# The last tile's output projection on its own plan of loads and operands

## Chip, core and metric

The kernel runs on one core of a Trainium2 chip. The metric is the device time of one execution in microseconds (us). The kernel before was timed three times: 2693.33 us in the median, 2690.28 to 2696.13. The engines are named as in the profile: PE multiplies matrices, DVE and ACT work on vectors, POOL on vectors too, SP issues DMA transfers.

## What is computed

Two mixers over 2048 rows of 1024 channels in float32: a gated MLP, then chunked attention with a shared K and V, a final output projection with a residual add, and an RMS norm. Only the last lines matter here:

```python
o = jnp.moveaxis(o, 0, 1).reshape(bsz, s, B_WIDTH)   # attention output, 16 heads of 64
return (o * jax.nn.silu(z)) @ w_out                  # gate, then output projection 1024 x 1024
...
x = x + chunk_attention_mixer(...)                   # residual
return rms_norm(x, final_norm_g)                     # final norm
```

## The kernel before

**Tiles.** The 2048 rows are four tiles t = 0..3 of 512 rows. In the attention part a tile goes through eight head pairs p = 0..7, each pair through eight steps u (`score`, `flip`, and `value` for each head). The output projection of tile t is done while tile t + 1 goes through its pairs: it is PE's filler work between the steps. `ahead(t, p)` (L1617) hands out this filler in small steps, by the table `SHARE`: in pair 7 of tile 3 it gives the last 12 steps of tile 2's projection and then the first 13 of tile 3's. What is left of tile 3's projection runs alone at the very end (L1693).

**Precision.** Each float32 operand is split in a high and a low part (`fp32r`), and a product is three matmuls (`mm3`, L112): high x high, left high x right low, left low x right high, at L113, L114 and L115. `split_s` (L291) splits a left operand: ACT copies the high part (Sho), DVE subtracts (Slo).

**Strassen.** The projection of a tile is one level of Strassen: seven products in the order `PHS = (1, 7, 2, 6, 5, 4, 3)`, each for two row halves jp, so 14 products of 12 matmuls. One product is four steps of filler. `o_right` (L228) brings a product's weights (two tiles q, each a high and a low part of 512 KiB, from the DRAM tensor `ows`), for tile 3's products 2, 3 and 5 from unsplit tensors instead, with the split on ACT and DVE (`split_in`, L209 and L210). All weight tiles lie in the eight places of tag `T`; a product needs four, so a load waits until the product before last has finished. `strassen` (L260) asks for left operands one product ahead and, for tile 3, for weights one product ahead.

**Left operands of tile 3.** `last_open` (L1456) loads quarters `00`, `10`, `01`, `11` of the attention output, as far as they exist, and POOL forms the sums s1 to s4. The last pairs come straight from `last_og` (L1486), when `value` has ended; products 2, 5, 4, 3 and 6 need pair 7.

**Eviction.** `o_evict` (L1502) takes a finished product out of PSUM. Products 1 and 7 are copied to x and y tiles; 2 and 5 are added to residual half rows (`resid`, 256 KiB each), 6 changes x and y; 4 and 3 close a half row. `done` squares on ACT; when a row block b has both halves, `finish(b)` makes the norm factor (two DVE adds, a POOL power) and `scale` multiplies and stores. For tile 2 the rows go through DRAM (`x2d`) and come back into one place (`y`, tag `bx`); its `finish` and `scale` wait in the list `finals`, from which one is taken per step u of pair 7, the rest before the last projection runs (L1691).

**Order.** The order on each engine is laid down when the program is built, by a planner that ranks instructions by their place in the program and lets one go when its operands and a place for its result are there in the planner's own reckoning; `on_beat` and the like add an order edge by hand. SP issues its loads strictly in that order: one that waits holds up all behind it.

Of the kernel before, what the change touches and what calls it, by code (L numbers as in the profile page):

```python
# [33 lines left out]
def trunk_kernel(  # L34
# [193 lines left out]
    def o_right(t):  # L228
        def right(ph):
            out = []  # L230
            for q in range(2):
                name = f"bo{t}_{ph}_{q}"
                if t + 1 == NT and ph in (2, 3, 5):
                    raw = raw_w(t, f"raw_{name}")
                    w = [w_tile(f"w{i}_{name}") for i in "hl"]
                    nc.sync.dma_start(raw[:], owf[q][:] if ph == 5 else wb_out[1, ph - 2, q])
                    split_in(raw, *w)
                else:
                    w = [w_tile(f"w{i}_{name}") for i in "hl"]
                    for i in range(2):  # L240
                        nc.sync.dma_start(w[i][:].bitcast(F32), ows[ph, q][:, i, :])
                out.append(w)
            return out
        return right
# [46 lines left out]
    def split_s(pool, bufs, name, src):  # L291
        hi, lo = (
            pool.tile([P, 4, P], F32R, tag="S", name=f"S{i}{name}", bufs=bufs) for i in "hl"
        )
        nc.scalar.copy(hi[:], src)
        tv(lo[:], src, hi[:].bitcast(F32), op=sub)
        return [(hi[:, k, :], lo[:, k, :]) for k in range(4)]
# [920 lines left out]
    with ExitStack() as bctx:  # L1218
# [200 lines left out]
        def o_left(t):  # L1419
            a = {}  # L1420
            if t + 1 == NT:
                return last_left

# [62 lines left out]
        def last_og(p, og32, z):  # L1486
            k = p - 4
            o4 = og32[:].rearrange("p (j r s) -> p r j s", j=2, r=2)
            z4 = z[:].rearrange("p (j r s) -> p r j s", j=2, r=2)
            for r in range(2):  # L1490
                nc.vector.scalar_tensor_tensor(
                    v4(la[f"{r}1"])[:, k], o4[:, r], 0.5, z4[:, r], op0=ALU.mult, op1=ALU.mult
                )
            if p == 7:
                for f_ in last_sums(slice(768, 1024)):
                    f_()

        def last_left(ph, jp):
            n = {1: "00", 7: "s3", 2: "01", 6: "s2", 5: "s1", 4: "11", 3: "s4"}[ph]
            return split_s(sb, 4, f"o_{ph}_{jp}", v4(la[n])[:, :, jp, :])  # L1500

        def o_evict(t):  # L1502
# [7 lines left out]
            def place(r, c, jp):  # L1510
                if not last:
                    return c_tile(f"oc{t}_{r}{c}{jp}")[:]
                b = 2 * jp + r
                if b not in row:
                    row[b] = sb.tile([P, 2, 512], F32, tag="K", name=f"row{b}", bufs=4)
                return row[b][:, c, :]
# [17 lines left out]
            def finish(b):  # L1534
# [4 lines left out]
                if last:  # L1539
                    y = row[b]  # L1540
                else:
                    on_beat(first)
                    y = sb.tile([P, 2, 512], F32, tag="bx", name=f"y{t}_{b}", bufs=1)
                    nc.sync.dma_start(y[:].rearrange("p a b -> p (a b)"), x2d[t][b][:])

                def scale():
                    for c in range(2):
                        cs = slice(c * 512, c * 512 + 512)
                        ins = nc.vector.scalar_tensor_tensor(
                            y[:, c, :], y[:, c, :], r[:], gf[:, cs], op0=ALU.mult, op1=ALU.mult  # L1550
# [4 lines left out]
                        nc.sync.dma_start(out[r0 : r0 + P, cs], y[:, c, :])  # L1555
# [6 lines left out]
            def evict(ph, jp, ps):  # L1562
# [6 lines left out]
                if ph in (2, 5):  # L1569
                    r = 0 if ph == 2 else 1  # L1570
                    c = place(r, r, jp)
                    resid(r, r, jp, c)
                    tv(c, ps, c, op=add)
                    tg(c, c, x_ if ph == 2 else y_, op=add)
                    done(r, r, jp, c)
                    if ph == 5:
                        tv(x_, ps, x_, op=add)
                        for r, c, y in ((1, 0, y_), (0, 1, x_)):
                            o = c_tile(f"or{t}_{r}{c}{jp}")[:]
                            resid(r, c, jp, o)  # L1580
                            tg(y, y, o, op=add)
                elif ph == 6:
                    tv(x_, ps, x_, op=add)
                    tg(y_, y_, x_, op=add)
                else:
# [6 lines left out]
        def o_all(t):  # L1592
            yield from strassen(
                f"bo{t}", o_right(t), o_left(t), o_evict(t), (t + 1) // NT
            )

        outs = [o_all(t) for t in range(NT)]
# [19 lines left out]
        def ahead(t, p):  # L1617
# [8 lines left out]
            else:  # L1626
                if t + 1 < NT:
                    reload(t + 1)
                yield from some(outs[t - 1], SHARE[t][p])
# [61 lines left out]
        while finals:  # L1691
            finals.pop(0)()
# [58 lines left out]
```

## Time and profile before

| | us |
|---|---|
| median of three runs | 2693.33 |
| profiled execution | 2698.01 |
| its span | 2696.2 |
| PE busy in the span | 2627.2 |
| end of PE's last matmul, from the span's start | 2687.78 |

Times in the profile's rows count from the start of the span. A timeline row gives start, duration, engine, line and operation, output and inputs, and in brackets the idle time ahead of it with what ended it. A row of stages gives the stretch, its length, busy time of PE, PE's weight loads, DVE, ACT and POOL with the number of instructions, then the granted PE clock, the DMA engines' busy share and GB/s. `bo` is the PSUM tile of an output product, `wh_bo` and `wl_bo` its weights, `pv`, `tp` and `s` belong to the attention, `row` is a residual row block of tile 3, `or` a residual half row, `ou` an x or y tile.

### The profile page before, as it was taken

How to read it: one execution, taken by the hardware profiler on the slowest of the kernel's cores; microseconds unless marked ns; L12 is line 12 of the kernel's file. 1: busy time of each engine (PE TensorE's matmuls, PEld its weight loads, DVE VectorE, ACT ScalarE, POOL GpSimd, SP SyncE). 2: the span in 40 equal slices, each digit the busy share in tenths (PEclk: the TensorE clock that was granted, in tenths of full speed). 3: DMA queues.
4: the chain of work that ended last, by engine and by line, in shares of the span. 5: the costliest groups of instructions: out<-in, count | busy, mean ns of one | idle time of the engine just before them, and what ended most of it. 6: DMA issues, size and time to landing. Idle time of an engine off the chain costs nothing.

```text
span 2696.2 us, 38071 instructions
## 1 busy us (share of the span) xinstructions
PE 2627.2 (97%) x12960; PEld 2197.9 (82%) x12960; DVE 1892.0 (70%) x2937; ACT 1296.6 (48%) x2296; POOL 888.2 (33%) x874
## 2 busy tenths in 40 slices
PE   9999999999999999999989999999999999999997
PEld 7888888888888888888878788787887888788885
DVE  5655676766777568657677767788677667766676
ACT  5422242443434435333365466676556555655553
POOL 3511335152262414015043344343332223323243
PEclk9999999999999999999999999999999999999999
DMA  7898999989888879858666687788889667766576
GB/s 293 314 326 332 342 364 326 328 306 350 331 320 281 308 259 334 301 200 273 256 238 209 216 266 232 223 294 290 281 265 295 200 220 246 242 204 193 180 236 238
DMA packets 274770, 735.53 MB, mean 273 GB/s; under 512 B 29584, under 2 KB 61328, under 8 KB 274576
## 3 DMA queue, kind: packets, MB, share of 16 engines
q1 hardware_dynamic: 274576, 733.09, 79.2%
q8 instruction: 104, 1.70, 0.2%
q14 instruction: 90, 0.74, 0.1%
HBM read 540.56 MB, written 181.93 MB: 268 GB/s over the span
## 4 chain that ended last, share of the span: by engine, by line
PE 81%; DVE 7%; DMA 6%; issue 2%; ACT 2%; POOL 2%; SPq 1%; DVEq 0%; POOLq 0%; ACTq 0%
PE P L115 11%; PE P L114 11%; PE P L113 11%; PE pj L115 5%; PE pj L113 5%; PE pj L114 5%; PE pv L1391 4%; PE Po L113 4%; PE Po L114 4%; PE Po L115 4%; PE s L1331 4%; PE tp L1366 3%; PE vp L115 1%; PE vp L113 1%; PE vp L114 1%
## 5 line engine op out<-in xcount | busy, mean ns | idle before, releaser
L113 PE MATMUL P<-T,S 128*128 128x512 f32 x1248 | 497.0, 398 | 2.1 <-ACT S L393 2.1
L115 PE MATMUL P<-T,S 128*128 128x512 f32 x1248 | 491.1, 394 | 0.0
L114 PE MATMUL P<-T,S 128*128 128x512 f32 x1248 | 490.1, 393 | 0.6 <-DVE T L396 0.6
L1350 POOL TENSOR_SCALAR pr<-pr,sl 128x640 f32<-128x640 f32 (+4 forms) x256 | 199.3, 779 | 522.9 <-DVE sl L1349 473.8
L113 PE MATMUL pj<-hh_b,wh_b 128*128 128x512 f32 x768 | 320.6, 417 | 1.6 <-ACT hh_b L168 0.8
L115 PE MATMUL pj<-hh_b,wl_b 128*128 128x512 f32 x768 | 305.9, 398 | 0.8 <-DVE wl_b L210 0.7
L114 PE MATMUL pj<-hl_b,wh_b 128*128 128x512 f32 x768 | 304.4, 396 | 0.0
L1346 ACT ACTIVATE pr<-pr,nm 128x640 f32<-128x640 f32 (+4 forms) x256 | 195.4, 763 | 193.2 <-DVE nm L1339 182.4
L115 PEld LDWEIGHTS P<-T,S 128*128 128x128 f32 x1248 | 235.8, 189 | 50.4
L113 PEld LDWEIGHTS P<-T,S 128*128 128x128 f32 x1248 | 236.2, 189 | 46.9 <-ACT S L393 2.3
L114 PEld LDWEIGHTS P<-T,S 128*128 128x128 f32 x1248 | 236.0, 189 | 46.1 <-DVE T L396 1.0
L1371 DVE TENSOR_TENSOR pt<-tp,pt 128x640 fp32r<-128x640 f32 (+4 forms) x256 | 188.7, 737 | 49.2 <-ACT pt L1370 46.2
L1339 DVE CUSTOM_DVE_ANT_0 pr<-s,bias 128x640 f32<-128x640 f32 (+4 forms) x256 | 188.0, 735 | 43.6 <-PE s L1331 36.7
L1370 ACT CAST pt<-tp 128x640 fp32r<-128x640 f32 (+4 forms) x256 | 159.1, 622 | 50.9 <-PE tp L1366 47.3
L1366 PE MATMUL tp<-ident,pr 128*128 128x128 f32 x1120 | 167.8, 276 | 10.4 <-DVE pt L1371 7.9
L115 PEld LDWEIGHTS pj<-hh_b,wl_b 128*128 128x128 f32 x768 | 145.5, 189 | 34.1 <-DVE wl_b L210 2.8
L1366 PEld LDWEIGHTS tp<-ident,pr 128*128 128x128 f32 x1120 | 131.4, 141 | 44.6 <-issue 17.0
L113 PEld LDWEIGHTS pj<-hh_b,wh_b 128*128 128x128 f32 x768 | 146.5, 191 | 20.1 <-ACT wh_b L209 1.6
L1391 PEld LDWEIGHTS pv<-pt,V 128*128 128x128 f32 x896 | 144.2, 190 | 20.2 <-ACT pt L1370 2.6
L114 PEld LDWEIGHTS pj<-hl_b,wh_b 128*128 128x128 f32 x768 | 146.6, 191 | 17.1
L1391 PE MATMUL pv<-pt,V 128*128 128x256 f32 (+3 forms) x896 | 154.4, 321 | 2.7 <-ACT pt L1370 1.8
L210 DVE TENSOR_TENSOR wl_b<-raw_b,wh_b 128x1024 fp32r<-128x1024 f32 x96 | 125.8, 1311 | 26.9 <-ACT wh_b L209 25.3
(283 smaller groups left out, 5739.4 us busy)
## 6 DMA issues: line engine op xcount, KB each, us to landing
S<-hsd SPq DMA_DIRECT2D x288, 512.0 KB, 5.4
rw<-in_w_a SPq DMA_DIRECT2D x108, 512.0 KB, 6.3
A<-ytd SPq DMA_DIRECT2D x72, 512.0 KB, 5.8
raw_b<-wk SPq DMA_DIRECT2D x72, 512.0 KB, 4.4
hsd<-S SPq DMA_DIRECT2D x56, 512.0 KB, 4.3
V<-vhd SPq DMA_DIRECT2D x56, 512.0 KB, 5.7
wh_bo<-ows SPq DMA_DIRECT2D x50, 512.0 KB, 4.7
wl_bo<-ows SPq DMA_DIRECT2D x50, 512.0 KB, 5.8
```

Source lines behind the costliest of these rows:

```text
L113: first = mm(ps, lh, rh, start=first, stop=False)
L114: mm(ps, lh, rl, start=False, stop=False)
L115: mm(ps, ll, rh, start=False, stop=last)
L210: tv(wl[:], raw[:], wh[:].bitcast(F32), op=sub)
L1331: mm(ps[:, sg, :w], q[:, qb * P : (qb + 1) * P], kx[:, koff + sg * w : koff + (sg + 1) * w], start=i == 0, stop=i == 1,)
L1339: nc.vector.tensor_tensor_reduce(out=pr[:, c0:].rearrange("p (a b) -> p a b", a=nseg), in0=ps[:, :nseg, :w], in1=bias[:, c0:].rearrange("p ...
L1346: nc.scalar.activation(pr[:, c0:], pr[:, c0:], AF.Exp, scale=-1.0, bias=nm[:], accum_out=sl[:])
L1350: nc.gpsimd.tensor_scalar(pr[:, c0:], pr[:, c0:], sl[:], 1.0, op0=ALU.mult, op1=ALU.mult)
L1366: ins = tpose(tp[:, b, :], pr[:, b * P : (b + 1) * P], ident[:])
L1370: nc.scalar.copy(oh, tp[:, b0:5, :].rearrange("p a b -> p (a b)"))
L1371: nc.vector.tensor_tensor(pt[:, 2560 + o + b0 * P : 2560 + o + 640], tp[:, b0:5, :].rearrange("p a b -> p (a b)"), oh.bitcast(F32), op=ALU ...
L1391: mm(po[:, q0 * P : q1 * P], vtl[t, p][:, i, hs], rhs, start=(i == blocks[0] and j == 0), stop=(i == 7 and j == 1),)
```

## The change

Tile 3's projection leaves the shared `strassen` and gets a generator of its own, `last_all`, with a hand-written table of what is asked for at which product.

- Weights: products 1, 7, 6 and 4 stay in the `T` places. Product 5 goes into the two `V` places (free when `value` of pairs 6 and 7 has ended), product 3 into the one `PT` place (free after the last `value`), both from the split tensors, so with no `split_in`; product 2 alone is still loaded unsplit, and split into the four `raw` places. Product 1 is asked for six steps before tile 2's projection ends (`last_first`).
- Left operands are asked for two products ahead and lie in the eight `Q` places instead of four `S`. If product 2's first one is asked for before pair 7 is there, three quarters of it are split at once and the last when `last_og` has run (`owed`).
- The residual comes as four whole row blocks (512 KiB, `last_row`) into `K` places, asked for at the third and fourth of the 14 products. The block of quarter 11 gets its y at product 6 instead of at product 5.
- Tile 2's `finals` are no longer emptied before the last projection; what is left is taken one by one from the sixth of the 14 products on. Row block 0 of tile 2 comes back into two half places of tag `og`.

```diff
     def o_right(t):
...
-                if t + 1 == NT and ph in (2, 3, 5):
-                    raw = raw_w(t, f"raw_{name}")
-                    w = [w_tile(f"w{i}_{name}") for i in "hl"]
-                    nc.sync.dma_start(raw[:], owf[q][:] if ph == 5 else wb_out[1, ph - 2, q])
-                    split_in(raw, *w)
-                else:
-                    w = [w_tile(f"w{i}_{name}") for i in "hl"]
-                    for i in range(2):
-                        nc.sync.dma_start(w[i][:].bitcast(F32), ows[ph, q][:, i, :])
+                w = [w_tile(f"w{i}_{name}") for i in "hl"]
+                for i in range(2):
+                    nc.sync.dma_start(w[i][:].bitcast(F32), ows[ph, q][:, i, :])
...
-    def split_s(pool, bufs, name, src):
+    def split_s(pool, bufs, name, src, tag="S", parts=None):
...
+        def part(ks):
+            nc.scalar.copy(hi[:, ks], src[:, ks])
+            tv(lo[:, ks], src[:, ks], hi[:, ks].bitcast(F32), op=sub)
+
+        if parts is None:
+            part(slice(0, 4))
+        else:
+            part(slice(0, 3))
+            parts.append(lambda: part(slice(3, 4)))
...
             if p == 7:
+                closed.append(p)
+                while owed:
+                    owed.pop(0)()
                 for f_ in last_sums(slice(768, 1024)):
                     f_()
...
-            return split_s(sb, 4, f"o_{ph}_{jp}", v4(la[n])[:, :, jp, :])
+            return split_s(
+                sb, 8, f"o_{ph}_{jp}", v4(la[n])[:, :, jp, :], "Q",
+                owed if ph == 2 and not closed else None,
+            )
+
+        def last_right(ph, q):
+            name = f"bo_{ph}_{q}"
+            if ph == 5:
+                v = sb.tile([P, 8, 256], F32R, tag="V", name=f"w{name}", bufs=2)
+                w = [v[:, i * 4 : i * 4 + 4, :].rearrange("p a b -> p (a b)") for i in range(2)]
+            elif ph == 3:
+                if q == 0:
+                    lw["pt"] = sb.tile([P, 5376], F32R, tag="PT", name=f"w{name}", bufs=1)
+                w = [lw["pt"][:, (2 * q + i) * 1024 : (2 * q + i + 1) * 1024] for i in range(2)]
+            elif ph == 2:
+                w = [
+                    sh.tile([P, 1024], F32R, tag="raw", name=f"w{i}{name}", bufs=4)[:]
+                    for i in "hl"
+                ]
+            else:
+                w = [w_tile(f"w{i}{name}")[:] for i in "hl"]
+            if ph == 2:
+                raw = raw_w(NT - 1, f"raw_{name}")
+                nc.sync.dma_start(raw[:], wb_out[1, 0, q])
+                nc.scalar.copy(w[0], raw[:])
+                tv(w[1], raw[:], w[0].bitcast(F32), op=sub)
+            else:
+                for i in range(2):
+                    nc.sync.dma_start(w[i].bitcast(F32), ows[ph, q][:, i, :])
+            lw[ph, q] = w
+
+        def last_row(b):
+            row[b] = sb.tile([P, 2, 512], F32, tag="K", name=f"row{b}", bufs=4)
+            nc.sync.dma_start(
+                row[b][:].rearrange("p a b -> p (a b)"), x1d[NT - 1][b * P : (b + 1) * P, :]
+            )
+
+        def last_first():
+            for q in range(2):
+                last_right(1, q)
+            lviews[0] = last_left(*ltodo[0])
+
+        def last_all():
+            plan = {
+                0: ((2, 0), (2, 1)), 1: ((5, 0),), 2: ((6, 0), (6, 1), (0, None), (2, None)),
+                3: ((5, 1), (1, None), (3, None)),
+                4: ((4, 0), (4, 1)), 5: ((3, 0), (3, 1)),
+            }
+            evict = o_evict(NT - 1)
+            for q in range(2):
+                last_right(7, q)
+            lviews[1] = last_left(*ltodo[1])
+            for i, (ph, jp) in enumerate(ltodo):
+                ps = pmm.tile([P, 512], F32, tag="mm", name=f"bo_{ph}_{jp}")
+                vs = lviews.pop(i)
+                for k in range(4):
+                    hi, lo = lw[ph, k // 2]
+                    c = slice((k % 2) * 512, (k % 2) * 512 + 512)
+                    ins = mm3(ps[:], *vs[k], hi[:, c], lo[:, c], k == 0, k == 3)
+                    if closed and k == 3:
+                        beat.append(ins.ins.name)
+                        if finals and i > 4:
+                            finals.pop(0)()
+                    if k == 1:
+                        for m in plan.get(i, ()):
+                            if m[1] is None:
+                                last_row(m[0])
+                            else:
+                                last_right(*m)
+                        if i + 2 < len(ltodo):
+                            lviews[i + 2] = last_left(*ltodo[i + 2])
+                    if k < 3:
+                        yield
+                evict(ph, jp, ps[:])
+                yield
...
+                elif t + 2 == NT and b == 0:
+                    on_beat(first)
+                    y = [half_tile("og", f"y{t}_{b}_{c}", 2)[:] for c in range(2)]
+                    for c in range(2):
+                        nc.sync.dma_start(y[c], x2d[t][b][:, c * 512 : c * 512 + 512])
...
-                    resid(r, r, jp, c)
+                    if not last:
+                        resid(r, r, jp, c)
                     tv(c, ps, c, op=add)
-                    tg(c, c, x_ if ph == 2 else y_, op=add)
+                    if not (last and ph == 5):
+                        tg(c, c, x_ if ph == 2 else y_, op=add)
...
                     tg(y_, y_, x_, op=add)
+                    if last:
+                        c = place(1, 1, jp)
+                        tg(c, c, y_, op=add)
...
-        outs = [o_all(t) for t in range(NT)]
+        outs = [o_all(t) for t in range(NT - 1)] + [last_all()]
...
+                if t + 1 == NT:
+                    yield from some(outs[t - 1], SHARE[t][p] - 6)
+                    last_first()
+                    yield from some(outs[t - 1], 6)
+                else:
+                    yield from some(outs[t - 1], SHARE[t][p])
...
-        while finals:
-            finals.pop(0)()
         run(outs[NT - 1])
```

35 lines of the change are left out of this document (17 added, 18 removed).

## The prediction

> **What bounds the kernel now.** I read the page first, then the stages of the last 100 us, then TensorE's (PE's) own timeline there.
>
> ```profile
> span 2696.2 us, 38071 instructions
> PE 2627.2 (97%) x12960; PEld 2197.9 (82%) x12960; DVE 1892.0 (70%) x2937; ACT 1296.6 (48%) x2296; POOL 888.2 (33%) x874
> ```
>
> PE is busy 97% of the span, so nearly everywhere a saved DMA or vector instruction is worth nothing: only PE's idle time and its slow clock can be won. Both gather at the end, from 2608 us on. PE's timeline, the rows with an idle time in front, then two rows that give the pace, then PE's last matmul:
>
> ```profile
> 2612.41 0.77 PE L113 MATMUL bo<-wh_bo,Sho 128*128 128x512 f32 x1 [3.52 <-DMA wh_bo<-ows]
> ...
> 2625.07 0.74 PE L1391 MATMUL pv<-pt,V 128*128 128x512 f32 x2 [0.64 <-DVE rr_f L127]
> ...
> 2631.76 0.50 PE L113 MATMUL bo<-wh_bo,Sho 128*128 128x512 f32 x1 [1.60 <-DMA wh_bo<-ows]
> ...
> 2634.27 0.50 PE L114 MATMUL bo<-wl_bo,Sho 128*128 128x512 f32 x1 [0.28 <-DMA wl_bo<-ows]
> ...
> 2647.68 0.50 PE L113 MATMUL bo<-wh_bo,Sho 128*128 128x512 f32 x1 [1.41 <-ACT Sho L295]
> ...
> 2651.23 0.50 PE L115 MATMUL bo<-wh_bo,Slo 128*128 128x512 f32 x1 [2.52 <-DVE Slo L296]
> ...
> 2660.03 0.39 PE L114 MATMUL bo<-wl_bo,Sho 128*128 128x512 f32 x1
> 2660.25 0.39 PE L115 MATMUL bo<-wh_bo,Slo 128*128 128x512 f32 x1
> ...
> 2664.65 0.51 PE L115 MATMUL bo<-wh_bo,Slo 128*128 128x512 f32 x1 [0.84 <-DVE Slo L296]
> ...
> 2682.47 0.50 PE L115 MATMUL bo<-wh_bo,Slo 128*128 128x512 f32 x1 [3.74 <-DVE Slo L296]
> ...
> 2687.38 0.40 PE L115 MATMUL bo<-wh_bo,Slo 128*128 128x512 f32 x1
> ```
>
> Who is late: twice a weight, then the left operands (Sho, Slo). The stages round the long gaps carry the granted clock in the third column from the end:
>
> ```profile
> 2612.41:2618.14 5.73, 5.73 (x15) 4.70 (x16) 1.73 (x4) 0.92 (x2) 2.82 (x4) 0.50 0.99 396
> 2618.00:2624.00 6.00, 6.00 (x34) 5.00 (x33) 4.57 (x9) 3.95 (x8) 3.13 (x3) 0.99 0.08 33
> ...
> 2651.23:2656.00 4.77, 4.77 (x14) 3.81 (x15) 1.50 (x3) 0.62 (x1) 0.12 (x1) 0.64 0.92 277
> ...
> 2682.47:2687.78 5.31, 5.31 (x15) 3.88 (x15) 3.41 (x6) 0.49 (x3) 0.55 (x1) 0.68 0.34 125
> 2687.78:2696.20 8.42, 0.00 (x0) 0.00 (x0) 3.96 (x9) 1.10 (x4) 1.10 (x2) 0.62 0.33 125
> ```
>
> After each long gap the clock is 0.50 to 0.68 for about 5 us; a gap thus costs itself plus the slow stretch. The last stage is the tail behind PE's last matmul: 8.42 us.
>
> **What the idle time after 2625 is worth.** The first gap (3.52 us) and the 0.64 us belong to tile 2, whose product 3 asks for its weights where it did; I leave them alone. The others: 1.60 + 0.28 + 1.41 + 2.52 + 0.84 + 3.74 = 10.39 us. Slow clock: 4.77 x (1 - 0.64) = 1.72 and 5.31 x (1 - 0.68) = 1.70. A matmul is drawn 0.39 us long but the next starts 0.22 us later (the two pace rows), so every gap hides about 0.16 us more; six gaps, 0.96. Ceiling: 10.39 + 3.42 + 0.96 = **14.8 us**.
>
> **Term 1, weights of product 1 (1.88 + 0.32 us).** SP, the queue that issues all loads in order:
>
> ```profile
> 2574.90 4.05 SPq L236 DMA_DIRECT2D raw_bo<-in_wb_out  x2
> ...
> 2623.65 1.00 SPq L1555 DMA_DIRECT2D out<-y  x2
> ...
> 2626.12 0.41 SPq L241 DMA_DIRECT2D wh_bo<-ows  x1
> 2626.63 0.40 SPq L1544 DMA_DIRECT2D y<-x2d  x1
> 2627.12 0.38 SPq L241 DMA_DIRECT2D wl_bo<-ows  x1
> ...
> 2641.54 0.38 SPq L1544 DMA_DIRECT2D y<-x2d  x1
> ...
> 2665.76 7.48 SPq L1508 DMA_DIRECT2D or<-x1d  x4
> ```
>
> The second half of product 1's weights goes out at 2626.12, behind the store of tile 2's first finished rows, which waits for DVE until 2623.65; meanwhile the DMA engines move 33 GB/s (2618 to 2624). The change asks for all four pieces six steps earlier, ahead of that store in program order. Their T places are free once tile 2's product 4 ends, and 2 MiB at the 396 GB/s seen at 2612 take 5.3 us: landed by about 2619, before PE wants them at 2625. Worth the whole term.
>
> **Term 2, the hand-over from attention to product 2 (1.41 + 2.52 + 1.72 + 0.32 us).** The rows of ACT and DVE, each from its own timeline:
>
> ```profile
> 2645.16 0.58 ACT L1400 COPY ot<-pv 64x512 f32<-64x512 f32 x1 [2.43 <-PE pv L1391]
> ...
> 2647.01 1.14 ACT L295 CAST Sho<-A_hh 128x512 fp32r<-128x512 f32 x2
> ...
> 2658.06 0.19 ACT L1523 ACTIVATION_READ_ACCUMULATOR jk<-row 128x1 f32 x1
> ```
>
> ```profile
> 2645.77 0.69 DVE L1401 TENSOR_TENSOR og<-pv,ot 64x512 f32<-64x512 f32 x1 [3.04 <-ACT ot L1400]
> 2646.50 0.76 DVE L1491 SCALAR_TENSOR_TENSOR A_hh<-og,Z 128x256 f32<-128x256 f32 x2
> 2648.69 1.88 DVE L1549 SCALAR_TENSOR_TENSOR y<-y,rr_f,gf 128x512 f32<-128x512 f32 x2 [1.43 <-DMA y<-x2d]
> 2650.49 1.28 DVE L296 TENSOR_TENSOR Slo<-A_hh,Sho 128x512 fp32r<-128x512 f32 x2
> ...
> 2676.70 1.25 DVE L1537 TENSOR_TENSOR rr_f<-ssq 128x1 f32<-128x1 f32 x1
> ...
> 2678.81 2.41 DVE L1549 SCALAR_TENSOR_TENSOR row<-row,rr_f,gf 128x512 f32<-128x512 f32 x2 [0.66 <-POOL rr_f L128]
> ...
> 2681.74 0.68 DVE L296 TENSOR_TENSOR Slo<-A_hl,Sho 128x512 fp32r<-128x512 f32 x1
> ```
>
> Slo of product 2 was ready to run at 2647.6 and ran at 2650.49: in front of it DVE stood for a y row that SP had sent for only at 2641.54. Two edits hit this: the y of block 0 gets its own place, so its load isn't queued behind another's store; and three quarters of the first operand are split beforehand, so that only head pair 7's quarter is owed. From the copy at 2645.16 to the cast at 2647.01 are 1.85 us; the owed cast and subtraction (128x128) have no row. Below, a row 128x1 wide takes 0.19 us on ACT; above, the full 128x512 takes about 0.6 on each (half of the x2 rows). I take a quarter of the full pair and hand-overs, 0.7: the gate opens 2.5 us after 2645.16 (to 3.2). Cover: five matmuls of product 7 and nine of product 2 at 0.23 us, 3.2 us. Left over 0 to 0.3; charged **0.2**. If the cover is gone, the 2.5 us show as a gap.
>
> **Term 3, operands of products 5 and 3 (0.84 + 3.74 + 1.70 + 0.32 us).** At 2681.74 Slo stands in DVE's line behind the scaling of a finished row (2.41 us), that behind POOL's root, and that behind four residual adds whose rows SP sent for as late as 2665.76, 7.48 us long. The change removes those eight half-row loads for four whole ones, sent when K places come free; splits operands two products (5.5 us) ahead, so Slo is in front of the scaling; and drops four ACT casts and four L210 subtractions of weights. Worth the whole term, less what follows.
>
> **What is paid.** (a) Loads: products 5 and 3 now fetch 2 MiB each instead of 1, so 2 MiB more, 5.3 us of the DMA engines. From 2645 to the want of product 3's weights about 6.5 MiB have to land (half of 5, all of 4 and 3, y and its stores): 17 us at 396 GB/s, and eight products of 2.76 us (12 matmuls at 0.23), 22 us, lie between; all are sent for before the late y store. Charged 0. SP issues one DMA more in all, at 0.4 us, in a queue that isn't full. (b) Crowding of DVE and POOL, now the same adds in 26 us instead of 42:
>
> ```profile
> L1574 POOL TENSOR_TENSOR row<-row,ou 128x512 f32<-128x512 f32 x4 | 5.8, 1449 | 9.9 <-DVE row L1573 8.4 <-issue 1.4
> L1581 POOL TENSOR_TENSOR ou<-ou,or 128x512 f32<-128x512 f32 x4 | 5.8, 1466 | 1.3 <-DMA or<-x1d 1.3
> L1584 POOL TENSOR_TENSOR ou<-ou,ou 128x512 f32<-128x512 f32 x2 | 3.0, 1532 | 3.4 <-DVE ou L1583 3.4
> ...
> L210 DVE TENSOR_TENSOR wl_bo<-raw_bo,wh_bo 128x1024 fp32r<-128x1024 f32 x4 | 6.7, 1687 | 1.1 <-ACT wh_bo L209 1.1
> L296 DVE TENSOR_TENSOR Slo<-A_hl,Sho 128x512 fp32r<-128x512 f32 x6 | 5.1, 843 | 0.0
> ```
>
> POOL's ten adds are 14.6 us and run at nearly PE's pace (six products, 16.6 us), so product 4's eviction, which needs them, can be late; DVE loses 6.7 us of work. Bounds: 0, if all stays inside the two-product lead; 23 us, if sixteen POOL instructions (ten adds, three sums, three roots) each hold DVE and so PE for 1.45 us. Slo's mean of 0.84 against 0.68 free says the rows lie far nearer the low end. Charged **1.5**. [...] (c) The tail: four row finishes come in 8 us instead of 12; between 0 and 2.4 (one scaling in the way). Charged **0.3**.
>
> **Sum.** 14.8 - 0.2 - 1.5 - 0.3 = 12.8 us. The profiled execution took 2698.01 (span 2696.2, 1.8 around it), 4.7 over the median; 2698.0 - 12.8 = 2685.2 there, and 2693.3 - 12.8 = **2680.5 us** by the median. Its own range, with paid sums from 0 to 5, is 2678.5 to 2683.5.
>
> **Rivals.** *A wait for product 7's weights takes the place of product 1's.* If SP still stands until 2623.65, 5.5 MiB come at once (stores and y 1.5, product 5's half 1, rows 1, product 7 2): 14.5 us, to 2639, where PE wants them at 2625.1 + 5.5 (product 1) + 4.2 (values, two transposes and a score between, an estimate from the same timeline), 2634.8. A gap of 4.3 and 1.7 of slow clock: 2686.5. For it: SP did stand so. Against: the early loads can use the trough at 2618. *The plan isn't what runs*: SP's real order stays as late as now, and only the early operands count (1.41 + 2.52 + 1.72 + 0.32 - 2.0 = 4): 2689.3. For it: the planner already moves loads far from where they are written (product 2's raw weights leave at 2574.90, fifty us before product 1 begins). Against: places, not positions, held the late ones. *The first gap shrinks too* (3.52 + 5.73 x 0.50 + 0.16 = 6.5): 2674.0; against it, nothing asks for those weights sooner. *Slower: DVE and POOL become the bound.* Sixteen POOL instructions each hold the chain 1.45 us, 23.2 in all: 14.8 - 23.2, 2701.7. It decides from 0.9 us per instruction; for it speaks the 1.25 us row, against it the two-product lead.
>
> **Chances.** Forecast 0.60, product 7's wait 0.16, plan not run 0.10, first gap too 0.06, crowding 0.08. A measurement tells about 0.2% (5.4 us) from no change, so faster means under 2687.9: 0.60 + 0.06, most of the 0.16 and a little of the 0.10, 0.80. Slower 0.08; the rest, 0.12, within. The range reaches from 2674, the first gap gone, to 2692, the plan not run and one gap more; beyond lie the crowding and the edges.
>
> **What would show it.** Right: wh_bo of product 1 sent for before the first out<-y; no idle row of PE above 1 us after 2625, granted clock 1.00 from 2625 to PE's end, PE's last matmul near 2675 and 8 to 9 us behind it. Wrong: PE idle on wh_bo at product 7; Slo still behind L1549; rr_f and Slo rows of over 1 us with PE idle behind them; the gap at 2608.89 longer, by loads slipped in front of tile 2's last weights.

## The result, and the profile after

The changed kernel took **2679.3 us** in the median of five runs (2675.85 to 2687.32), the kernel before 2696.13 us in five runs beside it. The ratio is 0.9948 with a 95% interval of 0.9929 to 0.9968, 14 us of 2693. Forecast were 2680.5 us and a range of 2674 to 2692. The profiled execution took 2682.42 us. The first two lines of its page:

```profile
span 2680.6 us, 38054 instructions
...
PE 2616.2 (98%) x12960; PEld 2188.9 (82%) x12960; DVE 1885.4 (70%) x2934; ACT 1291.4 (48%) x2293; POOL 883.6 (33%) x874
```

PE's timeline of the changed kernel from the last matmul of tile 3's projection (`pj`) on: the rows with an idle time, in brackets at their end, and the last rows of `pj`, `pv` and `bo`.

```profile
2593.73 0.40 PE L115 MATMUL pj<-hh_b,wl_b 128*128 128x512 f32 x1
...
2608.86 0.73 PE L1368 MATMUL tp<-ident,pr 128*128 128x128 f32 x5 [1.00 <-DVE pt L1373]
2611.61 0.47 PE L113 MATMUL bo<-wh_bo,Sho 128*128 128x512 f32 x1 [2.01 <-ACT Sho L291]
...
2618.17 0.74 PE L1368 MATMUL tp<-ident,pr 128*128 128x128 f32 x5 [0.30 <-DVE pt L1373]
...
2622.21 0.50 PE L1393 MATMUL pv<-pt,V 128*128 128x512 f32 x1 [0.51 <-DVE rr_f L127]
...
2633.89 0.50 PE L114 MATMUL bo<-wlbo,Qho 128*128 128x512 f32 x1 [1.20 <-DMA wlbo<-ows]
...
2638.61 2.44 PE L1393 MATMUL pv<-pt,V 128*128 128x512 f32 x15
...
2669.71 0.39 PE L115 MATMUL bo<-wbo,Qlo 128*128 128x512 f32 x1
```

None of the six gaps that the prediction counts after 2625 us is left; a new one, 1.20 us, stands at product 7. The stages of the changed kernel (after the first gap; from the last `pv` to PE's end; the tail), then the first two of these in the kernel before:

```profile
2611.73:2617.73 6.00, 6.00 (x31) 4.79 (x31) 5.94 (x12) 3.52 (x8) 3.55 (x5) 1.00 0.98 367
2641.05:2670.10 29.05, 29.05 (x127) 23.13 (x125) 22.90 (x32) 10.71 (x24) 18.67 (x15) 1.00 0.90 344
2670.10:2680.60 10.50, 0.00 (x0) 0.00 (x0) 5.77 (x12) 1.34 (x4) 1.10 (x2) 0.72 0.44 167
```

```profile
2612.41:2618.41 6.00, 6.00 (x18) 4.97 (x19) 1.73 (x4) 0.92 (x2) 3.09 (x4) 0.52 0.96 384
2645.07:2687.78 42.71, 33.95 (x125) 24.80 (x124) 31.35 (x40) 15.53 (x29) 18.28 (x15) 0.92 0.65 232
```

The stretch that took 42.71 us with PE busy for 33.95 at a clock of 0.92 now takes 29.05, all of it busy at 1.00. Also new: no slow clock behind the first gap, and a longer tail, 10.50 us against 8.42.

**How the runs are compared.** Executions of the same code differ, by 12.4 us in one pair, already ahead of the stage that was changed (last section). So each profile is cut at three events that every one has: **A** from the start of the last `pj` matmul to the end of the last `pv`, **B** from there to PE's end, **C** the tail. They are read from rows like those above (after: 2593.73, 2641.05, 2670.10, 2680.60), from one execution of each kernel. The ratio compares whole executions, each kernel with runs of the kernel before that were timed beside it.

| kernel | ratio to before, 95% interval | A | B | C | sum |
|---|---|---|---|---|---|
| before | 1 | 50.8 | 42.7 | 8.4 | 102.0 |
| after | 0.9948 [0.9929, 0.9968] | 47.3 | 29.1 | 10.5 | 86.9 |
| u1_one_ahead | 0.9945 [0.9930, 0.9959] | 47.3 | 30.7 | 9.9 | 87.9 |
| u2_weights_in_T | 0.9961 [0.9945, 0.9976] | 47.1 | 31.3 | 9.4 | 87.8 |
| u3_ask_1_late | 0.9954 [0.9939, 0.9968] | 49.5 | 28.7 | 10.6 | 88.8 |
| u4_rows_late | 0.9979 [0.9967, 0.9990] | 47.2 | 36.7 | 11.8 | 95.7 |
| u5_split_5_and_3 | 0.9956 [0.9940, 0.9972] | 49.5 | 32.3 | 8.7 | 90.6 |
| u6_split_and_one_ahead | 0.9969 [0.9955, 0.9984] | 50.3 | 32.6 | 10.1 | 93.1 |
| v3_y0_in_bx | 0.9951 [0.9936, 0.9966] | 48.5 | 31.8 | 10.6 | 90.9 |
| v1_lead_alone | 0.9998 [0.9989, 1.0008] | 47.8 | 43.6 | 8.1 | 99.5 |
| v4_no_splits_alone | 0.9999 [0.9989, 1.0009] | 50.2 | 44.5 | 8.5 | 103.2 |
| m2_tail_order | 0.9930 [0.9911, 0.9949] | 48.4 | 29.8 | 8.4 | 86.6 |
| m3_A_loads_behind_weights | 0.9926 [0.9906, 0.9947] | 44.7 | 29.7 | 10.6 | 85.0 |
| m4_all_three | 0.9926 [0.9912, 0.9940] | 44.8 | 29.4 | 8.5 | 82.7 |

The u kernels and v3 take one part back from the changed kernel (u6 two), the v1 and v4 kernels put one part into the kernel before, the m kernels go on from the changed one. B repeats well: after, m2 and m3 ask for the loads and operands of B alike and have 29.1 to 29.8. A repeats less well: after, u1, u2, u4 and m2, whose edits concern what comes later, have 47.1 to 48.4. A difference in B under 1 us is not read.

### The profile page after: what moved, and what is told of

It is laid out like the page before. It is cut to its first block, busy times and chain, and to the rows that moved or that the text cites. A ratio compares the mean times of both kernels' runs of the same rounds, so it can differ in the third digit from the quotient of the medians.

```text
span 2680.6 us, 38054 instructions
## 1 busy us (share of the span) xinstructions
PE 2616.2 (98%) x12960; PEld 2188.9 (82%) x12960; DVE 1885.4 (70%) x2934; ACT 1291.4 (48%) x2293; POOL 883.6 (33%) x874
## 4 chain that ended last, share of the span: by engine, by line
PE 82%; DVE 8%; DMA 4%; issue 2%; ACT 2%; POOL 2%; SPq 0%; DVEq 0%; POOLq 0%; ACTq 0%
PE P L115 11%; PE P L114 11%; PE P L113 11%; PE pj L115 5%; PE pj L113 5%; PE pj L114 5%; PE pv L1393 4%; PE Po L115 4%; PE Po L113 4%; PE Po L114 4%; PE s L1333 4%; PE tp L1368 4%; PE vp L115 1%; PE vp L113 1%; PE vp L114 1%
## 5 line engine op out<-in xcount | busy, mean ns | idle before, releaser
L115 PEld LDWEIGHTS P<-T,S 128*128 128x128 f32 x1248 | 235.2, 188 | 50.3
L113 PEld LDWEIGHTS P<-T,S 128*128 128x128 f32 x1248 | 235.9, 189 | 47.1 <-ACT S L395 2.3
L1372 ACT CAST pt<-tp 128x640 fp32r<-128x640 f32 (+4 forms) x256 | 159.1, 622 | 48.1 <-PE tp L1368 44.5
```

Of the source, the lines that this page charges most:

```text
L113: first = mm(ps, lh, rh, start=first, stop=False)
L115: mm(ps, ll, rh, start=False, stop=last)
L1372: nc.scalar.copy(oh, tp[:, b0:5, :].rearrange("p a b -> p (a b)"))
```

## Experiments: one part taken back

**Operands one product ahead (u1).**

```diff
-            lviews[1] = last_left(*ltodo[1])
-                        if i + 2 < len(ltodo):
-                            lviews[i + 2] = last_left(*ltodo[i + 2])
+                        if i + 1 < len(ltodo):
+                            lviews[i + 1] = last_left(*ltodo[i + 1])
```

> The changed kernel with left operands asked for one product ahead instead of two; places, weights, rows and finals as changed. Theory (the lead hides the operands): gaps of PE ending at a Qlo or Qho come back at the hand-over to product 2 (1.5 to 3 us) and at products 5 to 3 (1 to 4 us), the span 3 to 7 us longer than the changed kernel's 2680.6. Rival (the lead is worth nothing, it was the eight late half-row loads and the four weight splits that held DVE): no such gap over 0.5 us, span within 1.5 us of 2680.6.

PE's one idle row in B, at the hand-over to product 2:

```profile
2637.22 0.50 PE L113 MATMUL bo<-whbo,Qho 128*128 128x512 f32 x1 [1.19 <-ACT Qho L291]
```

B is 1.7 us longer, of which this gap explains 1.2 and its hidden part 0.16. So the theory's gap at the hand-over came, smaller than its 1.5 to 3 us. Its gaps at products 5 to 3, where the kernel before had lost most, did not come: with rows and weights there in time, a lead of one product is enough there.

**Block 0's y back in bx (v3).**

```diff
-                elif t + 2 == NT and b == 0:
+                elif t + 2 == NT and b == 9:
```

> The changed kernel with the y rows of tile 2's block 0 back in bx, the one place that the other three blocks share; all else as changed. Counted from tile 3's last projection matmul (pj) to the end of the span, the changed kernel takes 86.9 us. Reading of the prediction (the own place keeps the scaling of a late row from standing in front of the split of product 2's operand): with three quarters of that operand split beforehand only a short piece is exposed, 87 to 90, with the loss at the hand-over to product 2. Rival (what counts is SP's line, in which a load of y waits for bx in front of weights): one more such wait, PE idle on weights of product 1, 7 or 2, 88 to 92. Second rival: the own place is worth nothing, 86.4 to 87.5.

PE's idle rows in B, and DVE's rows at the hand-over:

```profile
2645.30 0.50 PE L115 MATMUL bo<-whbo,Qlo 128*128 128x512 f32 x1 [1.49 <-DVE Qlo L292]
...
2660.26 0.50 PE L114 MATMUL bo<-wlbo,Qho 128*128 128x512 f32 x1 [0.49 <-DMA wlbo<-ows]
```

```profile
2641.49 0.86 DVE L292 TENSOR_TENSOR Qlo<-A_hh,Qho 128x128 fp32r<-128x128 f32 x1
2642.28 2.36 DVE L1636 SCALAR_TENSOR_TENSOR y<-y,rr_f,gf 128x512 f32<-128x512 f32 x2
2644.56 0.68 DVE L292 TENSOR_TENSOR Qlo<-A_hh,Qho 128x512 fp32r<-128x512 f32 x1
```

The scaling of the late y stands in front of a split again, as in the kernel before, this time of product 2's second operand. B grows by 2.7 us, of which the gap of 1.49 us and its hidden part are 1.65. The rival's wait, on weights of product 1, 7 or 2, did not come; the 0.49 us stand at product 4, where m2, without this edit, has 0.39. Of the 4.0 us in the sum another 1.1 are in A; m2 has the same A (48.4), and in both a slow clock followed the first gap (0.52 and 0.54). So the place of y is worth about 2.7 us, by the way that the first reading gave; the count of 90.9 lies just above that reading's 87 to 90.

**Products 5 and 3 in T places (u2).**

```diff
-            if ph == 5:
+            if ph == 55:
-            elif ph == 3:
+            elif ph == 33:
-                0: ((2, 0), (2, 1)), 1: ((5, 0),), 2: ((6, 0), (6, 1), (0, None), (2, None)),
-                3: ((5, 1), (1, None), (3, None)),
-                4: ((4, 0), (4, 1)), 5: ((3, 0), (3, 1)),
+                0: ((2, 0), (2, 1)), 2: ((6, 0), (6, 1), (0, None), (2, None)),
+                3: ((1, None), (3, None)),
+                4: ((5, 0), (5, 1)), 8: ((4, 0), (4, 1)), 10: ((3, 0), (3, 1)),
```

> The changed kernel with products 5 and 3 back in the T places (still 2 MiB each from the split tensors), asked for when the places come free. Theory (places, not bytes, made the loads late): 4's and 3's weights are asked for one product half after the places come free, 5.5 us before they are wanted, and 2 MiB take 5.3 us and about 1.5 us to start and land: gaps on the weights of about 1 to 2 us each at products 4 and 3, span 2 to 5 us longer than 2680.6. Rival (the V and PT places were not needed): no gap on weights there, within 1 us. Rival (loads collide and pile up): more than 8 us longer.

```profile
2657.50 0.71 PE L113 MATMUL bo<-whbo,Qho 128*128 128x512 f32 x2 [0.38 <-DVE ou L1666]
2658.76 0.50 PE L114 MATMUL bo<-wlbo,Qho 128*128 128x512 f32 x1 [0.55 <-DMA wlbo<-ows]
```

Both gaps stand at product 4; at product 3, where the theory had another, there is none. Its 1.5 us to start and land are an estimate; the store at 2623.65 in the kernel before, with the DMA engines idle ahead of it, lands 2.0 us after its issue (256 KB, 0.7 us at 396 GB/s), which leaves 1.3. B is 2.2 us longer, of which these gaps and their hidden parts are 1.25; the rest lies in no long idle row. The whole count is only 0.9 longer. The places, with the earlier requests that they allow, are thus worth one or two us, not a stage.

**Product 1's weights asked for as late as before (u3).**

```diff
             evict = o_evict(NT - 1)
+            last_first()
...
-                    yield from some(outs[t - 1], SHARE[t][p] - 6)
-                    last_first()
-                    yield from some(outs[t - 1], 6)
+                    yield from some(outs[t - 1], SHARE[t][p])
```

> The changed kernel with product 1's weights and first operand asked for after tile 2's last product, as before the change. Theory (term 1 of the prediction): SP stands at the store of tile 2's first finished rows again, half of product 1's weights leaves after 2620, PE waits 1.5 to 2.5 us on whbo at product 1; the gap near 2609 stays as it is in the changed kernel. Rival (the early ask is also what shortened the gap near 2609 from 3.52 us to 1.00 + 2.01): that gap goes back to 3.5 us with a granted clock of 0.5 behind it, and the span is 4 to 6 us longer. Rival (ask is moved up by the planner anyway): nothing changes.

PE's row at product 1 and SP's rows ahead of it:

```profile
2621.16 0.50 PE L113 MATMUL bo<-whbo,Qho 128*128 128x512 f32 x1 [0.69 <-DMA whbo<-ows]
```

```profile
2613.62 1.00 SPq L1643 DMA_DIRECT2D out<-y  x2
...
2617.31 0.38 SPq L1535 DMA_DIRECT2D whbo<-ows  x1
```

Half of product 1's weights stand behind `out<-y` again, as in the kernel before, but PE waits 0.69 us and not the 1.5 to 2.5 expected. A is 2.2 us longer than in the changed kernel. This execution had a slow clock behind the first gap (0.51 over 6 us, against 1.00 in the changed kernel); against m2 and v3, where it was 0.54 and 0.52, A is 1.1 longer. That is the fairer comparison: the early request is worth about 1.1 us. The first gap stays in two pieces (0.75 + 2.86 us), so the early request is not what split it.

**Residual rows asked for at the eviction (u4).**

```diff
-                0: ..., 2: ((6, 0), (6, 1), (0, None), (2, None)),
-                3: ((5, 1), (1, None), (3, None)),
+                0: ..., 2: ((6, 0), (6, 1)),
+                3: ((5, 1),),
...
-                return row[2 * jp + r][:, c, :]
+                b = 2 * jp + r
+                if b not in row:
+                    last_row(b)
+                return row[b][:, c, :]
```

> The changed kernel with the four whole residual rows asked for where they are first used instead of two products ahead. The time counted is that from tile 3's last projection matmul (pj) to the end of the span: 101.96 us before, 86.87 changed. The planner leaves rows 0 and 2 where they are and sends rows 1 and 3 behind the store of tile 2's last y. Theory now (loads that stand behind a store in SP's line are what cost before): POOL's add of row 11 and DVE's evictions of product 5 wait for the row, PE loses 2 to 5 us, counted time 89 to 92. Rival (PSUM's four tiles and the operands split ahead absorb it): within 1 us of 86.87.

```profile
2669.78 0.76 PE L113 MATMUL bo<-wbo,Qho 128*128 128x512 f32 x1 [5.25 <-issue]
```

```profile
2655.64 1.64 SPq L1645 DMA_DIRECT2D out<-y  x2
2658.14 1.61 SPq L1543 DMA_DIRECT2D row<-x1d  x2
```

```profile
2667.09 1.26 POOL L1682 TENSOR_TENSOR row<-row,ou 128x512 f32<-128x512 f32 x1 [9.54 <-DMA row<-x1d]
```

```profile
2668.39 0.69 DVE L1664 TENSOR_TENSOR row<-bo,row 128x512 f32<-128x512 f32 x1 [8.14 <-POOL row L1682]
2669.00 0.68 DVE L1669 TENSOR_TENSOR ou<-bo,ou 128x512 f32<-128x512 f32 x1
```

The last two rows are sent for behind product 3's weights and the store of a scaled y, as the half rows stood behind such a store in the kernel before. POOL's add waits for a row, DVE's eviction of product 5 for that add, and PE stops for 5.25 us at the start of product 3 ("issue": no releaser is shown). It goes on 0.10 us after DVE's second read of product 5's first result. So it seems to have waited for the place of that result, one of the four in PSUM (tag `mm`). B grows by 7.7: this gap, one of 0.87 us on product 6's weights, and a slow stretch behind the long gap, with matmuls starting 0.43 us apart up to 2672.47 and 0.23 us apart after it. The whole count is 95.7, above the theory's 89 to 92. Of the parts taken back this one costs most. The loads are as large as in the changed kernel, so it is when they are sent that counts here; what their size is worth no run shows.

**The splits of 5 and 3 put back (u5), and that with one product's lead (u6).** u6 has u1's edit as well.

```diff
-            if ph == 2:
+            if ph in (2, 3, 5):
-                nc.sync.dma_start(raw[:], wb_out[1, 0, q])
+                nc.sync.dma_start(raw[:], owf[q][:] if ph == 5 else wb_out[1, ph - 2, q])
```

> The changed kernel with products 5 and 3 loaded unsplit again (1 MiB each instead of 2) into their V and PT places and split on ACT and DVE: four casts of 1.05 us, four subtractions of 1.2 us or more. Theory now (in the run with the lead alone the gaps moved to exactly these splits, 4.41 us on the cast and 2.36 us on the subtraction of product 3): DVE's line is late again at products 5 and 3, counted time 2 to 6 us above 86.87. Rival (the cost there was the late load of the unsplit weights, not the split: here they are loaded into places that come free early): within 1 us.

> Both undone: products 5 and 3 loaded unsplit and split on ACT and DVE, left operands one product ahead. Theory (each part covers for the other, so one undone costs little and two undone cost more than their sum): one-ahead alone cost 1.0 us of the counted time; together 4 to 8 us above 86.87. Rival (parts add up): the split run's figure plus 1.0.

PE's idle rows in B, u5:

```profile
2651.10 0.50 PE L114 MATMUL bo<-wbo,Qho 128*128 128x512 f32 x1 [1.39 <-DVE wbo L1532]
...
2664.37 0.50 PE L114 MATMUL bo<-wbo,Qho 128*128 128x512 f32 x1 [0.98 <-DVE wbo L1532]
```

DVE's subtractions of weights now end the waits; B is 3.2 us longer with them and 3.6 with both edits. A is longer as well, by 2.2 and 3.0. In u5 the first half of product 5's weights is split so early that DVE does it in the middle of the first gap, ahead of `pt`:

```profile
2602.55 2.29 DVE L1532 TENSOR_TENSOR wbo<-raw_bo,wbo 128x1024 fp32r<-128x1024 f32 x1
```

PE's idle time there is 3.84 + 0.97 us (u6: 4.17 + 1.44), and the clock in the 6 us behind the first of the two is 0.58 (0.57). The split thus costs in both stages, 3.7 us in the sum, inside the theory's 2 to 6.

Whether the lead and the splits cover for each other stays open. By the sum, in which the expectation was put, u6 loses 6.2 us, inside the theory's 4 to 8 and more than the 1.0 + 3.7 of the parts; by B it loses 3.6, less than their 1.7 + 3.2. What is more in the sum lies in A and in the tail, where one execution of each does not decide.

## Experiments: one part alone in the kernel before

**The two-product lead (v1).** `strassen` gets a parameter, and the operands go to the eight Q places, with product 2's first in two parts as in the changed kernel.

```diff
-    def strassen(name, right, left, evict, look):
+    def strassen(name, right, left, evict, look, far=1):
...
+        if far == 2:
+            ready(1)
...
-                    ready(i + 1)
+                    ready(i + far)
```

> The kernel before with one part of the change alone: tile 3's left operands two products ahead in the Q places, with the owed quarter. Theory (terms 2 and 3 of the prediction come from the operands): the gaps of 1.41, 2.52, 0.84 and 3.74 us and the two slow stretches of 1.7 us go, in all 8 to 11 us of the 16; the gap of 1.60 us on product 1's weights stays. Rival (loads and rows were what held DVE and SP, the operands merely showed it): less than 4 us, gaps move to weights of products 2, 5 or 3.

The stage B of this kernel, PE's idle rows in it, and SP's rows that lead to the last two:

```profile
2640.47:2684.08 43.61, 34.50 (x125) 25.94 (x124) 29.79 (x43) 15.46 (x30) 18.44 (x16) 0.84 0.66 227
```

```profile
2646.17 0.50 PE L115 MATMUL bo<-wh_bo,Qlo 128*128 128x512 f32 x1 [1.77 <-DVE Qlo L300]
...
2664.34 0.73 PE L113 MATMUL bo<-wh_bo,Qho 128*128 128x512 f32 x2 [0.58 <-DMA wh_bo<-ows]
...
2672.62 1.22 PE L113 MATMUL bo<-wh_bo,Qho 128*128 128x512 f32 x2 [4.41 <-ACT wh_bo L209]
...
2676.19 0.79 PE L114 MATMUL bo<-wl_bo,Qho 128*128 128x512 f32 x1 [2.36 <-DVE wl_bo L210]
```

```profile
2660.25 5.10 SPq L1527 DMA_DIRECT2D or<-x1d  x4
2665.39 0.91 SPq L236 DMA_DIRECT2D raw_bo<-in_wb_out  x2
```

The lead did what it is for. The hand-over lost 1.41 + 2.52 us before and loses 1.77 now, and Slo of products 5 and 3 (0.84 and 3.74 us) is late nowhere. But product 3's raw weights leave SP behind the late residual rows, and then have to be split: 4.41 and 2.36 us. The idle time of B is 9.1 us (1.77 + 0.58 + 4.41 + 2.36) where the kernel before has 8.8 (1.41 + 2.52 + 0.84 + 0.25 + 3.74). So the rival came true, and the theory's 8 to 11 us did not: the ratio is 0.9998, and the 2.4 us by which the count is shorter lie in A.

**No splits of 5 and 3, their weights in T places (v4).**

```diff
-                if t + 1 == NT and ph in (2, 3, 5):
+                if t + 1 == NT and ph == 2:
```

> The kernel before with one part alone: products 5 and 3 load the split weights (2 MiB each) into the T places, no splits on ACT and DVE. Theory (places and SP's order still make them late): the 3.74 us gap at product 3 turns into gaps on the weights of products 5 and 3 of 1 to 4 us each, counted time between 97 and 103 against 101.96. Rival (the splits alone held DVE): the gaps of 0.84 and 3.74 us and the slow stretch vanish, counted time 94 to 96.

```profile
2643.27:2687.75 44.48, 35.22 (x125) 25.86 (x124) 25.15 (x36) 11.48 (x25) 19.07 (x15) 0.88 0.77 266
```

```profile
2677.62 0.70 PE L113 MATMUL bo<-wh_bo,Sho 128*128 128x512 f32 x2 [1.37 <-DMA wh_bo<-ows]
...
2680.86 0.78 PE L114 MATMUL bo<-wl_bo,Sho 128*128 128x512 f32 x1 [2.55 <-DMA wl_bo<-ows]
```

DVE is 6 us less busy than in the kernel before (25.15 against 31.35), and B is not shorter: now the weights themselves are late at product 3. The count of 103.2 lies at the theory's upper bound; the rival, which gave the splits alone the blame, fell. B's idle time is 9.1 us again (the two rows above, 3.02 at the hand-over, and 0.58, 0.88 and 0.69 on Slo). So at product 3 three chains (left operand, split, load of the weights) ended within a few us of each other; taking one away shows the next.

## Experiments: what the changed kernel still loses

**Order of the last finishes (m2).** A scaling is ordered behind the next block's add of epsilon.

```diff
-                root(r[:])
+                eps = root(r[:])
...
-                    scale()
+                    if held:
+                        held.pop(0)(eps)
+                    held.append(scale)
+                    if b == 2:
+                        held.pop(0)()
```

> The changed kernel with only the order of DVE's last instructions changed: the scaling of a finished block stands behind the add of epsilon of the next block, so that DVE does not wait for POOL's root with other work behind it. The changed kernel's tail (from PE's last matmul to the end of the span) is 10.5 us against 8.4 in the kernel before. If that excess is DVE's last evictions standing behind a scaling that waits for POOL: tail 8.0 to 9.0, counted from pj 84.5 to 85.5. Rival (the excess is POOL's own adds, late by the crowding): tail 10 to 11, counted 86.5 to 87.5.

DVE's last rows in the changed kernel, then in m2:

```profile
2669.89 1.41 DVE L1636 SCALAR_TENSOR_TENSOR row<-row,rr_f,gf 128x512 f32<-128x512 f32 x2 [0.66 <-POOL rr_f L128]
2671.22 1.28 DVE L1683 TENSOR_TENSOR row<-bo,ou 128x512 f32<-128x512 f32 x2
...
2676.10 1.42 DVE L1636 SCALAR_TENSOR_TENSOR row<-row,rr_f,gf 128x512 f32<-128x512 f32 x2 [0.66 <-POOL rr_f L128]
```

```profile
2670.73 0.69 DVE L1697 TENSOR_TENSOR row<-bo,ou 128x512 f32<-128x512 f32 x1 [0.44 <-PE bo L115]
...
2673.17 2.73 DVE L1638 SCALAR_TENSOR_TENSOR row<-row,rr_f,gf 128x512 f32<-128x512 f32 x4
```

In the changed kernel the last eviction stands behind a scaling that waits for POOL, in m2 it follows PE's end (2670.69) at once. The tail is 8.4 us, as expected; the sum gains only 0.3, because in this execution a slow clock (0.54) followed the first gap (A + 1.1) and B was 0.8 longer. The pair m3 and m4 below shows the same step, 10.6 to 8.5. Without the edit the tail is not always 10.5 either: it is 8.7 in u5, where PE ends later and DVE is through with more of its work by then.

**Loads of A behind tile 2's last weights (m3), and three edits together (m4).**

```diff
             def third():
+                loads()
...
-            return [third] + last_sums(slice(0, 512)) + [lambda: all_of(slice(512, 768))]
+            return [lambda: None, third] + last_sums(slice(0, 512)) + [lambda: all_of(slice(512, 768))]
```

`loads` holds the four loads of A that ran at once before. m4 is m2 and m3, and gives the own y place to block 3 (`b == 3` where the changed kernel has `b == 0`).

> The changed kernel with the four loads of A_hh and its neighbours (raw places, for tile 3's first operands) moved behind the weights of tile 2's product 3 in SP's order. The idle time before product 3 of tile 2, 1.00 + 2.01 us in the changed kernel and 3.52 us with a slow clock behind in the kernel before, is what the prediction left alone. If SP's line makes it (weights that leave at 2604.0 behind loads that wait for their places): those 3 us shrink to under 1, counted from pj 83.5 to 85.5. Rival (with the weights there in time the operand Sho from ACT or pt from DVE ends the wait at the same point): 86.4 to 87.5, the idle row still there and put down to ACT or DVE. Second rival: the later A loads delay the first operands of tile 3: 87.5 to 90.

> The changed kernel with three edits: the own place goes to the y rows of block 3 and not of block 0 (so that no load of y waits for bx in front of product 7's weights), the A_hh loads stand behind the weights of tile 2's product 3, and the last scalings stand behind the next block's add of epsilon. If each gain is what its own place in the trace shows (1.2 of idle time at product 7, about 3 before product 3 of tile 2, about 2 in the tail): counted from pj 80 to 83, the median 4 to 7 us under the changed kernel's. Rival (as with the parts that were taken back singly, each chain covers for another, and the gains don't add): counted 84 to 86, the median 1 to 3 us under.

The first idle rows of stretch A in m3, whose last `pj` matmul starts at 2581.30:

```profile
2598.35 0.50 PE L114 MATMUL bo<-wl_bo,Sho 128*128 128x512 f32 x1 [0.22 <-DMA wl_bo<-ows]
2605.07 0.74 PE L1368 MATMUL tp<-ident,pr 128*128 128x128 f32 x5 [1.41 <-DVE pt L1373]
```

The first gap, 3.0 us, is down to 0.22; waits of the attention (1.41, and 1.00 further on) come in its place, the wait at product 7 is not there, and A gains 2.6. In m4 A is m3's (44.8) and C is m2's (8.5), B is as before the edits (29.4), and the count is 82.7 against 86.9 and 102.0, inside the 80 to 83 that adding the single gains gave. The third edit, block 3's own place, was not run alone, and no gain of it shows: m3 has the same A without it. m4's median is 2673.62 us against 2694.96 for the kernel before beside it: **0.9926** (0.9912 to 0.9940). That m4 beats the changed kernel rests on the counted 4.2 us of one execution each; the intervals of the two ratios still overlap, and by the medians m4 can't be told from m2 (2674.84) or m3 (2673.40).

## Why the prediction was right, and where it wasn't

The sum was -12.8 us; the profiled spans differ by 15.6 and the counted stretches by 15.1. By stretch: A -2.2 forecast (term 1), -3.5 found; B -12.6 + 1.7 = -10.9 forecast (terms 2 and 3 less the hand-over's 0.2 and the crowding's 1.5), -13.7 found; C +0.3 forecast, +2.1 found. Of the signs of being right, two failed: one idle row after 2625 is above 1 us (1.20), and 10.5 us and not 8 to 9 lie behind PE's last matmul. That matmul ends at 2670.10, earlier than the 2675 named.

- **Term 1 (2.2) held in its cause.** SP sends product 1's weights from 2612.98 on, ahead of `out<-y`, and the gaps of 1.60 and 0.28 us are gone. Asked for late again (u3), they cost about 1.1 us, half of the term.

```profile
2612.98 0.39 SPq L1535 DMA_DIRECT2D whbo<-ows  x1
...
2620.05 1.00 SPq L1642 DMA_DIRECT2D out<-y  x2
...
2625.53 0.32 SPq L1630 DMA_DIRECT2D y<-x2d  x1
2625.94 0.38 SPq L1535 DMA_DIRECT2D wlbo<-ows  x1
```

- **The rival of product 7 came true in small.** By the last two rows three of the four pieces of product 7's weights (the first left at 2622.27) go out behind a load of y: a gap of 1.20 us instead of the 4.3 the rival gave, with no slow clock behind (1.00 from there to PE's end). Where PE came later by a slow clock behind the first gap (u1, u2, u3, u4, m2, v3: 0.51 to 0.72), no gap stands there.
- **Term 2 held.** Both its edits are needed: the lead takes the hand-over to 1.77 us (v1; with a shorter lead 1.19 comes back, u1), the place of y the rest (v3: 1.49 comes back).
- **Term 3's gaps went, but not by the part it names.** The prediction hung the 3.74 us on Slo and named the lead as what puts it in front of the scaling. The lead alone gives nothing in time (v1), nor does dropping the splits (v4); u1 shows the lead not needed at 5 and 3; u4 shows the early rows worth 7.7. What was missing in that step is that the row with the bracket names the last to arrive: behind it stood the next chain, and in v1 and v4 B had 9.1 us of idle time where the kernel before had 8.8. The sum came right since the change treated all chains at once. What the early rows alone would give in the kernel before was not run.
- **Crowding (1.5) was not paid.** DVE was held: Qlo, 0.68 us when free, takes 1.77 beside a POOL add, below; but PE doesn't wait for it after 2634. Qlo ends 0.54 us after the add, and free rows of its size start 0.60 us apart. The rival's row of 1.25 us, `rr_f` at 2676.70 in the kernel before, is of the same kind: it ends at 2677.95, POOL's adds beside it at 2677.94, and at 2683.47 the same add takes 0.15. The rival (sixteen such holds, each one in PE's way) fell: there are such rows, but no idle row of PE stands behind them. That each of the sixteen holds DVE and PE for 1.45 us was the author's estimate, which no run shows.

```profile
2657.92 1.77 DVE L292 TENSOR_TENSOR Qlo<-A_hl,Qho 128x512 fp32r<-128x512 f32 x1
```

```profile
2657.41 1.74 POOL L1679 TENSOR_TENSOR row<-row,ou 128x512 f32<-128x512 f32 x1
```

- **The tail (0.3) was mis-sized**: 2.1 was paid, near the bound of 2.4, and by what that bound named, one scaling in the way (m2, and m4 against m3).
- **"I leave them alone" failed for the first gap.** Two early splits (Qlo, from 2604.69 on) stand ahead of `pt` on DVE, so five transposes now fall into the gap (1.00 + 2.01 us instead of 3.52), and the clock behind stayed at 1.00, which saves the slow stretch of 5.73 x 0.50 = 2.9 us. The prediction had this only as a rival, by another way. It is also luck: in seven other kernels with the gap in two pieces the clock behind was 0.51 to 0.76 (last section). Product 7's wait took 1.4 us back.

So the forecast was right with errors that offset each other: A gave 1.3 and B 2.8 us more than forecast, the tail took 1.8 more. Of B's 2.8, 1.7 are charges that were not paid, 0.25 is an idle row at 2672.66 that the sum left out, and for the rest, about 0.9, no cause is shown: between the two slow stretches that it counted the clock was 1.00 (2656 to 2682.47). That the median came within 1.2 us of 2680.5 is luck too: the five executions lie between 2675.85 and 2687.32.

## What to carry to other kernels

An idle row names the last of several late inputs; before booking the whole gap for one edit, look when the other inputs of the same instruction arrived, for the second latest sets what the edit is worth. In a queue that issues in order, a load that is wanted soon goes ahead of a store that waits for a late result; here the late place cost 7.7 us of B, and the shorter lead 1.7. Count a stage between events that every version has, when whole executions scatter by more than the effect.

## What was not expected of the hardware

**The clock behind a gap in two pieces was 1.00 after 3.01 us of idle time and 0.54 after 3.75.** In eight kernels the first gap has about 0.7 us of transposes in it. Its two pieces come to 3.01 us in after, 3.12 in v1, 3.40 in u2, 3.54 in u4, 3.56 in u1, 3.61 in u3, 3.65 in v3 and 3.75 in m2. The granted clock in the 6 us from the restart is 1.00, 0.76, 0.72, 0.72, 0.72, 0.51, 0.52 and 0.54, in the same order. Two of these stretches, u1 and m2:

```profile
2605.64:2611.64 6.00, 6.00 (x24) 4.89 (x25) 4.23 (x9) 2.55 (x7) 4.11 (x5) 0.72 0.99 360
```

```profile
2611.04:2617.04 6.00, 6.00 (x19) 5.02 (x20) 3.90 (x9) 1.86 (x5) 3.76 (x5) 0.54 1.01 373
```

The idle time is not all of it: behind a gap in one piece the clock was 0.52 after 3.52 us (before) and 0.72 after 3.60 us (v4). What else sets it is not shown, nor whether the transposes between two pieces count as idle: no run separates that.

**The scatter of whole executions goes with the clock only in part.** m2's four runs went from 2669.64 us at a mean granted clock of 0.995 to 2680.86 at 0.991; 0.4% of 2680 is 10.7 us, of the 11.2 between them. But the changed kernel's own runs of 2675.85 and 2687.32 us both have 0.992. It can arise before the stage: the last `pj` matmul starts 12.4 us earlier in m3's profile (2581.30) than in the changed kernel's (2593.73), in code that is the same. Why they differ there stays open.
